# A hybrid encoder block on one Trainium2 core: 26 pairs of input projection blocks by one level of Strassen's recursion, in a stage of their own ahead of the DeltaNet heads

## Chip, core and metric

The kernel runs on one core of one Trainium2 chip. A core has TensorE (PE, matrix products), VectorE (DVE), ScalarE (ACT), GpSimd (POOL) and SyncE (SP), which here only issues DMAs; each works through its own queue of instructions in order, and waits on semaphores for the others. The metric is the device time of one execution in microseconds (us), lower is better.

## The reference, cut to what matters

x is 1024 tokens by 1024 channels, everything in float32. The input projection makes ten groups of 1024 channels (and 32 small ones for decays):

```python
h = rmsnorm(x, norm_w[l]) * (1.0 + scale[:, None, :]) + shift[:, None, :]
proj = h @ w_in[l]
(a_bg, a_cg, a_x, a_z, q, k, v, z_b, a_raw, b_raw, gate_a_raw, gate_b_raw) = jnp.split(proj, split_pts, axis=-1)
ya = a_cg * dwconv_centred(a_bg * a_x, conv_a_w[l])
ya = (ya * jax.nn.silu(a_z)) @ w_pa[l]
...
o = gated_delta_chunked(q2, k2, v2, g2, b2)     # 8 heads, both directions, chunks of 64 tokens
...
yb = (o * jax.nn.silu(z)).reshape(bsz, slen, VAL_DIM).astype(dt_) @ w_pb[l]
merged = jax.nn.sigmoid(gate_a_raw) * ya + jax.nn.sigmoid(gate_b_raw) * yb
x = x + gate[:, None, :] * (merged @ w_o[l])
return rmsnorm(x, final_norm_w)
```

q, k and v go through a convolution of width 5, SiLU and (q, k) a normalisation before the heads.

## The kernel before, in words

**Products.** Each group of 1024 channels is eight blocks of 128, so the projection has 80 blocks. A float32 operand is split into a high part (a cast to fp32r on ACT) and a low part (operand minus high part), and a product is three matmuls: high by high, high by low, low by high. A block is 2 halves of 512 tokens x 8 slices of the inner dimension x 3 = 48 matmuls of 128x128 by 128x512. The weights of a block come as two loads (wr), two casts on ACT (wh) and two subtractions on POOL (wl). The hidden h stands in SBUF as hhi and hlo.

**Stages.** A prologue loads x and the adaLN weights, normalises, transposes, and makes the products of q, k, v of head 0 and k of head 1. Then come the eight heads, then the mixer's remaining blocks ("the ax stage", lines 1113 to 1158: bg, ax, cg of each slice, a convolution of width 3, and directly yhi and ylo), then the products with w_pa, w_pb and w_o.

**A head.** `prep_k(h)` transposes k, loads two tiles D (a row of decays, broadcast over 128 partitions, one tile for each direction), subtracts, takes the exponential, multiplies with the gram matrix into N, collects its 32x32 diagonal blocks by DMA through DRAM into the tile E, and inverts them on POOL in 30 steps of two operations (`et<-E` and `E<-E,et`); DMAs bring the result back (s, N, Vb). `prep_q(h)` makes the q side and turns v into vp. `chain(h)` completes the inversion on TensorE (psy, psu, psz, psv) and then goes through eight steps, each of which is a chain of small matmuls (cb, o) and operations on DVE (r, S) and ACT (vw, vn). `head_out(h)` normalises the output, multiplies with silu(z) and stores it in yb_d. D, N, qg, ktok have two buffers each: `prep_k(h)` asks for `chain_e` of head h-2 first, because D of head h-2 is an operand of its last o matmul.

**Fill.** While heads wait, TensorE works on projection blocks. The generator `fill()` hands them out, chosen by `choose()`: k, q, v of the coming heads and z when what they need is done, and otherwise one of 24 gate blocks (ga, gb, az), whose activated results go to DRAM. There are 52 such blocks in the heads.

**Order.** A scheduler written in Python (`Scheduler`, `Engine`) runs while the program is built: it estimates costs and hops between engines, and so fixes the order of instructions of every engine through the prologue and the heads. Nothing is decided at run time: an engine waits for the next instruction in its list. Engines other than TensorE are recorded in line 278, TensorE in line 200. After the heads, the order of the code stands, with a few priorities (`tc.high_priority`).

Of the kernel before, what the change touches and what calls it, by code (L numbers as in the profile page):

```python
# [8 lines left out]
F32 = mybir.dt.float32  # L9
# [15 lines left out]
START = 6  # L25
RESERVE = 4
HOPS = {'same': 0.15, 'other': 0.2, 'from pe': 0.4, 'to pe': 0.35}
# [6 lines left out]
LO_POOL = (2, 5)  # L34

# [7 lines left out]
class Slot:  # L43
    """What was done to a part of a tile: ends of reads, writes and memsets, and instructions not issued yet."""
# [6 lines left out]
class Scheduler:  # L51
    """Orders the instructions of all engines by an estimate of when they can run.

    Instructions of the engines other than TensorE are kept until their operands are there by the estimate, and then
    go to their engine by priority. Streams are generators that ask for TensorE instructions, PSUM banks, tiles and
    each other's marks; the first of them goes on whose next instruction can start at once, or else the one that can
    start first."""
# [126 lines left out]
    def step(self, stream):  # L184
        """Does what a stream asks for, and goes on to what it asks for next."""
# [65 lines left out]
class Engine:  # L251
    """Hands an engine's instructions to the scheduler."""
# [31 lines left out]
def block(ctx: ExitStack, tc: tile.TileContext, x, cT, wada, wadag, badaT, nwT, win, wab, cva, cvq,  # L284
# [10 lines left out]
    wp = pool("wp", 2)  # L295
# [22 lines left out]
    sza_d = dr.tile([8, P, T], F32, name="sza_d")  # L318
    sgb_d = dr.tile([8, P, T], F32, name="sgb_d")
    yb_d = dr.tile([8, P, T], F32, name="yb_d")  # L320
# [25 lines left out]
    def kmul(ps, w, k, half):  # L346
        wh, wl = (t[:, ch(k)] for t in w)
# [5 lines left out]
    weights, wanted, early = {}, [], {}  # L353
# [36 lines left out]
    ctx.enter_context(tc.manual_schedule(engines={nc.tensor.engine}))  # L390
    hctx = ctx.enter_context(ExitStack())
# [8 lines left out]
    gctx = ctx.enter_context(ExitStack())  # L400
    gctx.enter_context(tc.manual_schedule(engines={e.engine for e in (nc.vector, nc.scalar, nc.gpsimd, nc.sync)}))
    gc_ = gctx.enter_context(tc.tile_pool(name="gc", bufs=1))
# [9 lines left out]
    xpads = [gc_.tile([P, T + 4], F32, name=f"xpad{i}") for i in range(2)]  # L412
    for xp in xpads:
        G.memset(xp[:, 0:2], 0.0)
        G.memset(xp[:, T + 2 : T + 4], 0.0)
# [6 lines left out]
    with tc.tile_pool(name="st", bufs=1) as st:  # L422
# [34 lines left out]
        xnT = st.tile([P, KT, T], F32, name="xnT")  # L457
# [113 lines left out]
        def hidden():  # L571
            for k in range(KT):
                hx = yield tile_of(st, [P, T], "hx", f"hx{k}", 2)
# [5 lines left out]
                for half in range(n):  # L579
# [4 lines left out]
                    with urgent():  # L584
                        V.tensor_scalar(hx[:, sl], xnT[:, k, sl], mod[:, 2 * k : 2 * k + 1], mod[:, 2 * k + 1 : 2 * k + 2],
# [26 lines left out]

        def first_products():
            banks = yield from outer(((po, "k0"), (pp, "q0")))
            for i, name in enumerate(("k0", "q0")):
                for half in range(2):
                    S.activation(xpads[i][:, 2 + 512 * half : 514 + 512 * half], banks[name, half], AF.Copy)
                    yield free(banks[name, half])
# [19 lines left out]
        def next_products():  # L638
            yield "need", "x"
            banks = yield from outer(((pc, "v0"),))  # L640
            early["v0"] = [banks["v0", half] for half in range(2)]
            yield want(win[Q0 + 1], "q1")
            yield "need", ("w", "k1")
            early["k1"] = []
            for half in range(2):
                early["k1"].append((yield from product_of("k1", half, po)))
# [49 lines left out]
        sched.run([loads(), modulate(), hidden(), norm_x(), first_products(), decay_product(), decays(), next_products(), first_weights(), loader(0, 2)])  # L696
# [15 lines left out]

    npad = [0]
    tiles = {}

    def conv(h, name, ct0, tag, bufs, ready=None):
        xp = xpads[npad[0] % 2]
        npad[0] += 1
        for half in range(2):
            if ready is None or ready:  # L720
                ps = ready[half] if ready else (yield from product_of(f"{name}{h}", half))
# [8 lines left out]
    def activated(name, j, dst_d, func):  # L730
# [7 lines left out]
        Q.dma_start(dst_d[j], xp[:, 2 : T + 2])  # L738

    def silu_z(h):  # L740
        sz = yield big("tmp", f"sz{h}", 2)
        for half in range(2):
            ps = yield from product_of(f"z{h}", half)
            with urgent():
                S.activation(sz[:, ch(half, 512)], ps, AF.Silu)
            yield free(ps)
        tiles["z", h] = sz
        yield "mark", ("z", h)
# [278 lines left out]
    def head_out(h):  # L1027
        yield ("need", ("chain", h))
        yield ("need", ("z", h))
        sz, os_ = tiles["z", h], ghead[h]["vp"]  # L1030
# [9 lines left out]
    def fill():  # L1040
        jobs = []
        for h in range(H):
            if h > 1:
                jobs.append((K0 + h, f"k{h}", conv(h, "k", 8, "kT", 3), [("chain_e", h - 3)] if h >= 3 else []))
            if h > 1:
                jobs.append((Q0 + h, f"q{h}", conv(h, "q", 0, "qT", 3), [("chain_e", h - 3)] if h >= 3 else []))
            if h:
# [292 lines left out]
```

## Time and profile before

| | |
|---|---|
| times of three runs | 1515.09, 1521.39, 1522.44 us; median 1521.39 |
| profiled execution: span | 1511.0 us |
| what the median has around this span | 10.4 us |
| prologue up to the end of k1's product | 106.6 us |
| heads with their fill | to 965 us |
| ax stage | 965 to 1229 us |
| w_pa, w_pb, w_o stages | 1229 to 1319, to 1407, to 1511 us |

The profile page names busy time of each engine over the span (PE is TensorE's matmuls, PEld its weight loads), and the chain of waits followed back from the last instruction. A group of instructions is a line of the code, an engine, an operation and the tiles it writes and reads ("out<-in"), with its count, busy us, mean ns of one, and the idle time ahead of it. A tile's view gives the min, median and max duration of each kind of instruction in ns, and the first and last start in us. The windows view gives the busy time of all engines in stretches of the span.

### The profile page before, as it was taken

The numbers are of one execution on the slowest core, as the hardware profiler recorded it, in microseconds if no ns is written. First come the engines' busy times: TensorE is split into PE (matmuls) and PEld (weight loads), VectorE is DVE, ScalarE is ACT, GpSimd is POOL, SyncE is SP. The second block draws the span as 40 slices with busy tenths as digits, with TensorE's granted clock in tenths as the row PEclk, the third lists the DMA queues.
The fourth block names the chain that finished last, engine by engine and source line by source line (L and its number), as shares of the span: only waits on it lengthen the run. The fifth ranks groups of instructions, "written<-read, shape, count | busy, mean of one in ns | idle before, by whom it ended". The sixth has DMA issues, their size and how long they took to land.

```text
span 1511.0 us, 22593 instructions
## 1 busy us (share of the span) xinstructions
PE 1433.0 (95%) x8730; PEld 1196.2 (79%) x8730; DVE 735.0 (49%) x1382; ACT 549.8 (36%) x1308; POOL 645.2 (43%) x793
## 2 busy tenths in 40 slices
PE   5999999898999999989999999999999999999898
PEld 3787878787787878878878878888888888888686
DVE  7869334664853845647628422134443344122325
ACT  5226325663553654635535424211111112122211
POOL 6213894167184392671852931222222222355401
PEclk7899999999999999999999999999999999999999
DMA  8232332223314113222132121322222137344602
GB/s 327 83 109 64 112 98 57 71 70 98 84 44 134 35 56 127 57 78 84 59 103 70 57 84 44 125 97 80 74 86 96 56 120 256 133 130 143 229 20 98
DMA packets 90298, 149.15 MB, mean 99 GB/s; under 512 B 41424, under 2 KB 41808, under 8 KB 90192
## 3 DMA queue, kind: packets, MB, share of 16 engines
q1 hardware_dynamic: 89904, 146.94, 29.6%
q8 instruction: 68, 1.11, 0.3%
q10 hardware_dynamic: 288, 0.79, 0.1%
q14 instruction: 38, 0.31, 0.1%
HBM read 118.21 MB, written 29.49 MB: 98 GB/s over the span
## 4 chain that ended last, share of the span: by engine, by line
PE 54%; DVE 9%; POOL 8%; ACT 5%; DMA 4%; issue 2%; SPq 0%; POOLq 0%; ACTq 0%
PE pp_az L200 4%; PE pp_gb L200 3%; PE cb L200 3%; PE pp_k L200 3%; DMA mr<-m_d 2%; PE o L200 2%; POOL E L278 2%; PE pp_v L200 2%; POOL et L278 2%; PE pp_cg L1103 2%; PE pp_cg L1105 2%; PE pp_cg L1104 2%; PE pp_bg L1105 2%; PE pp_ax L1105 2%; PE pp_bg L1104 2%
## 5 line engine op out<-in xcount | busy, mean ns | idle before, releaser
L278 POOL TENSOR_TENSOR E<-E,et 64x30 f32<-64x30 f32 (+14 forms) x240 | 143.9, 600 | 17.1
L278 POOL TENSOR_TENSOR et<-E 64x30 f32<-64x30 f32 (+14 forms) x240 | 135.2, 564 | 17.2
L1138 DVE TENSOR_TENSOR axp<-pp_ax,bg 128x512 f32<-128x512 f32 x16 | 11.1, 692 | 111.1 <-PE pp_ax L1105 90.5
L278 ACT ACTIVATE vw<-cb,cols 128x128 f32<-128x128 f32 x112 | 36.2, 365 | 76.1 <-PE cb L200 75.7
L278 ACT ACT_TABLE_LOAD x47 | 60.3, 1283 | 1.6 <-PEq L1335 0.8
L278 DVE SCALAR_TENSOR_TENSOR vT<-xpad,cvq_t,vT 128x1024 f32<-128x1024 f32 x32 | 58.6, 1831 | 1.0
L1095 POOL TENSOR_TENSOR wl_ax<-wr_ax,wh_ax 128x512 fp32r<-128x512 f32 x16 | 27.3, 1724 | 68.2 <-ACT wh_ax L1094 68.2
L278 POOL TENSOR_TENSOR wl_q<-wr_q,wh_q 128x512 fp32r<-128x512 f32 x16 | 22.0, 1390 | 72.2 <-ACT wh_q L278 67.4
L200 PE MATMUL pp_z<-hhi,wl_z 128*128 128x512 f32 x128 | 52.2, 408 | 0.0
L200 PE MATMUL pp_z<-hhi,wh_z 128*128 128x512 f32 x128 | 52.2, 407 | 0.0
L200 PE MATMUL pp_gb<-hlo,wh_gb 128*128 128x512 f32 x128 | 51.9, 406 | 0.0
L200 PE MATMUL pp_ga<-hhi,wh_ga 128*128 128x512 f32 x128 | 51.8, 405 | 0.0
L200 PE MATMUL pp_gb<-hhi,wh_gb 128*128 128x512 f32 x128 | 51.8, 405 | 0.0
L200 PE MATMUL pp_z<-hlo,wh_z 128*128 128x512 f32 x128 | 51.7, 404 | 0.0
L200 PE MATMUL pp_az<-hhi,wl_az 128*128 128x512 f32 x128 | 51.7, 404 | 0.0
L200 PE MATMUL pp_az<-hhi,wh_az 128*128 128x512 f32 x128 | 51.7, 404 | 0.0
L200 PE MATMUL pp_gb<-hhi,wl_gb 128*128 128x512 f32 x128 | 51.6, 403 | 0.0
L200 PE MATMUL pp_az<-hlo,wh_az 128*128 128x512 f32 x128 | 51.4, 402 | 0.0
L200 PE MATMUL pp_ga<-hlo,wh_ga 128*128 128x512 f32 x128 | 51.3, 401 | 0.0
L200 PE MATMUL pp_ga<-hhi,wl_ga 128*128 128x512 f32 x128 | 51.2, 400 | 0.0
L1104 PE MATMUL pp_pa<-ylo,wh_pa 128*128 128x512 f32 x128 | 50.8, 397 | 0.2 <-DVE ylo L1158 0.2
L1095 POOL TENSOR_TENSOR wl_pa<-wr_pa,wh_pa 128x512 fp32r<-128x512 f32 x16 | 21.9, 1388 | 68.1 <-ACT wh_pa L1094 68.1
(352 smaller groups left out, 4490.5 us busy)
## 6 DMA issues: line engine op xcount, KB each, us to landing
wada<-in_wada SPq DMA_DIRECT2D x16, 512.0 KB, 7.3
D<-gr_d SPq DMA_DIRECT2D x16, 512.0 KB, 5.9
xt<-in_x SPq DMA_DIRECT2D x8, 512.0 KB, 7.8
wr_k<-in_win SPq DMA_DIRECT2D x16, 256.0 KB, 2.6
wr_q<-in_win SPq DMA_DIRECT2D x16, 256.0 KB, 3.5
wr_v<-in_win SPq DMA_DIRECT2D x16, 256.0 KB, 2.6
wr_ga<-in_win SPq DMA_DIRECT2D x16, 256.0 KB, 2.9
qg<-er_d SPq DMA_DIRECT2D x8, 512.0 KB, 6.2
```

Source lines behind the costliest of these rows:

```text
L200: getattr(self.pe, what)(out, *ins, **kw)
L278: self._sched.record(self._name, lambda: real(*args, **kw), outs, ins, cost, extra, table, op == "memset")
L1095: G.tensor_tensor(lo[:, ch(q, 512)], raw, hi[:, ch(q, 512)].bitcast(F32), ALU.subtract)
L1103: PE.matmul(ps, wh, mhi[k][:, sl], start=k == 0, stop=False)
L1104: PE.matmul(ps, wh, mlo[k][:, sl], start=False, stop=False)
L1105: PE.matmul(ps, wl, mhi[k][:, sl], start=False, stop=k == KT - 1)
L1138: V.tensor_tensor(xp[:, 1 + 512 * half : 513 + 512 * half], ps, bg[:, ch(half, 512)], ALU.mult)
```

## The change

**Before the heads.** A new stage makes 26 pairs of blocks: four pairs of ga, three of gb, three of z, and for each of four positions a pair of bg, ax, cg and az. A pair is the product of 256 output channels with 1024 tokens, and is cut into 2x2 on each of its three dimensions: weights A11, A12, A21, A22 (slices of the inner dimension even or odd, since the rows of w_in are now laid out in the order KORDER), and B11 ... B22 of the hidden. The Winograd form of Strassen's recursion makes seven products of a quarter size in the place of eight: with the sums S1 to S4 of weights and T1 to T4 of the hidden, and sums of results. Each product is 4 slices x 3 = 12 matmuls, so a pair has 84 matmuls and not 96. For T1 to T4 the hidden is kept in float32 (xnT), and 16 sums on DVE, 16 casts on ACT and 16 low parts (11 on DVE, 5 on POOL) are made once. Each pair has 4 weight loads of 256 KB, 4 weight sums (DVE), seven casts (ACT) and seven low parts (POOL), made five products ahead (AHEAD). The results, activated, go to DRAM: sga_d, sgb_d, sz_d; and the mixer's whole result, after the convolution of width 3 and its multiplications, to y_d.

**Prologue.** The products of k0, q0, v0, k1 are copied to SBUF and stored to DRAM (raw_d), and loaded again as the heads start.

**Heads.** `fill()` has 24 blocks: q1, v1, and k, q, v of heads 2 to 7, and z and gb of positions 6 and 7 (TAIL) as spares. silu(z) is loaded from sz_d in `head_out`.

**After the heads.** The ax stage is gone. Eight tiles yr are loaded from y_d (two buffers), cast on ACT into yhi, and subtracted on DVE into ylo. The gate columns (wadag, ga) are made in the w_pa loop.

```diff
+    for m in range(4):
+        b11, b12, b21, b22 = (xnT[:, 2 * m + odd, ch(half, 512)] for odd in range(2) for half in range(2))
+        NV.tensor_tensor(b11, b12, b11, ALU.subtract)
+        NV.tensor_tensor(b12, b22, b12, ALU.subtract)
+        NV.tensor_tensor(b22, b22, b11, ALU.subtract)
+        NV.tensor_tensor(b21, b21, b22, ALU.subtract)
+        for n, t in zip(SUMS, (b22, b11, b12, b21)):
+            hi, lo = hop[n][m]
+            NS.activation(hi, t, AF.Copy)
+            (NG if lows % 3 == 2 else NV).tensor_tensor(lo, t, hi.bitcast(F32), ALU.subtract)
+            lows += 1
...
+    RHS = {"S2": "T2", "A11": "B11", "S1": "T1", "S3": "T3", "A12": "B21", "A22": "T4", "S4": "B22"}
...
+        def prep(self, n):
...
+            NS.activation(hi, t, AF.Copy)
+            NG.tensor_tensor(lo, t, hi.bitcast(F32), ALU.subtract)
+            self.ops[n] = hi, lo
+
+        def product(self, n):
...
+            for m in range(4):
+                mh, ml = hop[RHS[n]][m]
+                for i, (w, r) in enumerate(((hi, mh), (hi, ml), (lo, mh))):
+                    PE.matmul(ps, w[:, ch(m)], r, start=first and m == i == 0, stop=m == 3 and i == 2,
+                              skip_group_check=True)
+            self.after(n, ps)
...
+    pairs = [stored("ga", j, sga_d, AF.Sigmoid) for j in range(0, 8, 2)]
+    pairs += [stored("gb", j, sgb_d, AF.Sigmoid) for j in range(0, 8 - TAIL, 2)]
+    pairs += [stored("z", j, sz_d, AF.Silu) for j in range(0, 8 - TAIL, 2)]
+    pairs += [mixed(n, j) for j in range(0, 8, 2) for n in ("bg", "ax", "cg", "az")]
...
-        gates = [(G_A + j, f"ga{j}", activated("ga", j, sga_d, AF.Sigmoid), []) for j in range(8)]
-        gates += [(G_B + j, f"gb{j}", activated("gb", j, sgb_d, AF.Sigmoid), []) for j in range(8)]
-        gates += [(A_Z + j, f"az{j}", activated("az", j, sza_d, AF.Silu), []) for j in range(8)]
...
+        spare = [(Z0 + j, f"z{j}", activated("z", j, sz_d, AF.Silu), []) for j in range(8 - TAIL, 8)]
+        spare += [(G_B + j, f"gb{j}", activated("gb", j, sgb_d, AF.Sigmoid), []) for j in range(8 - TAIL, 8)]
...
-        yield from conv(0, "k", 8, "kT", 3, [])
+        yield from conv(0, "k", 8, "kT", 3, 0)
...
+    for k in range(KT):
+        raw = yp.tile([P, T], F32, tag="yr", name=f"yr{k}", bufs=2)
+        Q.dma_start(raw, y_d[k])
+        S.activation(yhi[k], raw, AF.Copy)
+        V.tensor_tensor(ylo[k], raw, yhi[k].bitcast(F32), ALU.subtract)
```

Three places show how the order moves. The first is ACT's list after the last product of the prologue, k of head 1 (pp_k). Before (xpad is the padded input of the convolution, wh the high part of a weight block, kT and qT the convolved k and q of head 0, ktp k's transposes):

```order
L278 ACTIVATE xpad_116<-v_1_721 128x512
L278 ACTIVATE wh_ga_889<-wr_ga_0_891 128x512
L278 ACTIVATE xpad_117<-pp_k_0_816 128x512
L278 ACTIVATE xpad_117<-pp_k_1_853 128x512
L278 ACT_TABLE_LOAD
L278 ACTIVATE kT_885<-kT_885 128x1024
L278 ACTIVATE wh_ga_889<-wr_ga_1_892 128x512
L278 ACTIVATE qT_886<-qT_886 128x1024
```

Now (raw is the copy for DRAM; T1h to T4h are the high parts of the sums of the hidden, whS and whA those of the weight sums and weights):

```order
L280 ACTIVATE raw_867<-pp_k_1_840 128x512
L728 ACTIVATE T2h_882<-xnT 128x512
L728 ACTIVATE T1h_890<-xnT 128x512
L728 ACTIVATE T3h_898<-xnT 128x512
L728 ACTIVATE T4h_906<-xnT 128x512
L728 ACTIVATE T2h_884<-xnT 128x512
...
L728 ACTIVATE T3h_904<-xnT 128x512
L728 ACTIVATE T4h_912<-xnT 128x512
L762 ACTIVATE whS_ga_984<-S_ga_982 128x512
L762 ACTIVATE whA_ga_988<-wr_ga_976 128x512
L762 ACTIVATE whS_ga_994<-S_ga_992 128x512
```

The casts of all sixteen sums stand between the copy of k1 and the first weight sum of the stage.

The second is TensorE's list in the last head's chain, in a late step. Before (cb, o: the chain's matmuls, pp_az: a fill block):

```order
L200 MATMUL cb7_0_8553<-r7_0_6_8784,N0_7_7517 128x128 [waits DVE_49]
L200 MATMUL cb7_1_8554<-r7_1_6_8786,N1_7_7518 128x128 [waits DVE_49]
L200 MATMUL pp_az4_1_8743<-hhi4_505,wl_az4_8426 128x512
L200 MATMUL pp_az4_1_8743<-hhi5_544,wh_az4_8425 128x512
L200 MATMUL pp_az4_1_8743<-hlo5_545,wh_az4_8425 128x512
L200 MATMUL pp_az4_1_8743<-hhi5_544,wl_az4_8426 128x512
L200 MATMUL pp_az4_1_8743<-hhi6_583,wh_az4_8425 128x512
L200 MATMUL pp_az4_1_8743<-hlo6_584,wh_az4_8425 128x512
L200 MATMUL pp_az4_1_8743<-hhi6_583,wl_az4_8426 128x512
L200 MATMUL cb7_0_8553<-vw7_0_6_8794,ktok7_7512 128x128 [waits Activation_49]
L200 MATMUL cb7_1_8554<-vw7_1_6_8796,ktok7_7512 128x128 [waits Activation_49]
L200 MATMUL o7_1_8552<-vn7_0_6_8797,D0_7_7515 128x128
```

Now:

```order
L202 MATMUL cb7_0_11114<-vw7_0_5_11247,ktok7_10033 128x128 [waits Activation_49]
L202 MATMUL cb7_1_11115<-vw7_1_5_11249,ktok7_10033 128x128 [waits Activation_49]
L202 MATMUL o7_1_11113<-vn7_0_5_11250,D0_7_10036 128x128
L202 MATMUL o7_0_11110<-vn7_1_5_11251,D1_7_10037 128x128
L202 MATMUL cb7_0_11114<-S7_0_5_11257,kT7_9780 128x128 [waits DVE_49]
L202 MATMUL cb7_1_11115<-S7_1_5_11259,kT7_9780 128x128 [waits DVE_49]
L202 MATMUL o7_1_11113<-S7_0_5_11257,qg0_7_10416 128x128
L202 MATMUL o7_0_11110<-S7_1_5_11259,qT7_9968 128x128
L202 MATMUL cb7_0_11114<-r7_0_6_11265,N0_7_10038 128x128 [waits DVE_49]
L202 MATMUL cb7_1_11115<-r7_1_6_11267,N1_7_10039 128x128 [waits DVE_49]
```

No fill matmul stands between the steps of head 7 any more; in the loops of the other heads there are 48 to 96.

The third is SP's list of DMAs at the end of the heads. Before (the store of the last head, then weights of the ax stage):

```order
L278 DMA yb_d<-sz_8424 128x1024
L278 DMA sza_d<-xpad_117 128x1024
L1093 DMA wr_bg_0_9092<-in_win 128x512
L1093 DMA wr_bg_1_9096<-in_win 128x512
L278 DMA sza_d<-xpad_116 128x1024
L1093 DMA wr_ax_0_9154<-in_win 128x512
L1093 DMA wr_ax_1_9158<-in_win 128x512
L278 DMA sza_d<-xpad_117 128x1024
```

Now (yr: the mixer's result, ybr: the heads', sga and sgb: gates):

```order
L280 DMA yb_d<-sz_10878 128x1024
L1275 DMA wr_pa_1_11590<-in_wpa 128x512
L280 DMA sz_11307<-sz_d 128x1024
L280 DMA yb_d<-sz_11307 128x1024
L1297 DMA yr_11367<-y_d 128x1024
L1297 DMA yr_11371<-y_d 128x1024
L1316 DMA wadag_11432<-in_wadag 128x1024
L1318 DMA sga_11434<-sga_d 128x1024
L1331 DMA ybr_11498<-yb_d 128x1024
L1318 DMA sga_11514<-sga_d 128x1024
L1331 DMA ybr_11580<-yb_d 128x1024
L1368 DMA sgb_12117<-sgb_d 128x1024
```

The loads of the mixer's result stand behind the last head's store, in turns with others.

More of the change, by code (lines that the diff above doesn't have):

```diff
@@ L615, in first_products @@
             for i, name in enumerate(("k0", "q0")):
-                for half in range(2):
-                    S.activation(xpads[i][:, 2 + 512 * half : 514 + 512 * half], banks[name, half], AF.Copy)
-                    yield free(banks[name, half])
+                yield from spill(i, banks, name)
         def decay_product():
@@ new lines, in block @@
+    tctx = ExitStack()
+    tctx.enter_context(tc.manual_schedule(engines=others))
+    tp = tctx.enter_context(tc.tile_pool(name="tp", bufs=1, reuse_waits="tile"))
+    bw = tctx.enter_context(tc.tile_pool(name="bw", bufs=1, reuse_waits="tile"))
+    SUMS = ("T2", "T1", "T3", "T4")
+    hop = {}
+    for i, n in enumerate(SUMS):
+        hop[n] = [[tp.tile([P, 512], F32R, name=f"{n}{p}{m}") for p in "hl"] for m in range(4)]
+    for n, odd, half in (("B11", 0, 0), ("B21", 1, 0), ("B22", 1, 1)):
+        hop[n] = [[t[2 * m + odd][:, ch(half, 512)] for t in (hhi, hlo)] for m in range(4)]
@@ L711, in conv5 @@
         S.activation(dst, dst, AF.Silu)
+    xpads = [gp.tile([P, T + 4], F32, name=f"xpad{i}") for i in range(2)]
+    for xp in xpads:
+        G.memset(xp[:, 0:2], 0.0)
+        G.memset(xp[:, T + 2 : T + 4], 0.0)
     npad = [0]
@@ L718, in conv @@
         npad[0] += 1
-        for half in range(2):
-            if ready is None or ready:
-                ps = ready[half] if ready else (yield from product_of(f"{name}{h}", half))
+        if ready is not None:
+            Q.dma_start(xp[:, 2 : T + 2], raw_d[ready])
+        else:
+            for half in range(2):
+                ps = yield from product_of(f"{name}{h}", half)
                 with urgent():
@@ L737, in activated @@
             yield free(ps)
[L738 to L748, printed above, removed]
+        Q.dma_start(dst[j], xp[:, 2 : T + 2])
+        yield "mark", (name, j)
     ghead = {}
@@ new lines, in block, with gate_column @@
+    bctx = ExitStack()
+    bp = bctx.enter_context(tc.tile_pool(name="bp", bufs=1, reuse_waits="tile", side="right"))
+    bhi = [bp.tile([P, T], F32R, name=f"bhi{k}") for k in range(KT)]
+    blo = [bp.tile([P, T], F32R, name=f"blo{k}") for k in range(KT)]
+    psm = bank(pc, "psg")
+    gsum = []
+    def gate_column(j):
+        PE.matmul(psm[:, j : j + 1], gsum[j], one)
+        V.tensor_tensor(gcol[:, j : j + 1], psm[:, j : j + 1], badaT_t[:, 16 + j : 17 + j], ALU.add)
+    with tc.tile_pool(name="bs", bufs=2, reuse_waits="tile", side="right") as bs:
@@ L1140, in block @@
-            V.tensor_scalar(acc, xp[:, 0:T], cva_t[:, j, 0:1], None, ALU.mult)
-            for i in range(1, 3):
-                V.scalar_tensor_tensor(acc, xp[:, i : i + T], cva_t[:, j, i : i + 1], acc, ALU.mult, ALU.add)
-            ga = ap.tile([P, P], F32, tag="ga", name=f"ga{j}")
+                ps = product(w, yhi, ylo, half, f"pa{j}")
+                V.tensor_tensor(sg[:, ch(half, 512)], ps, sg[:, ch(half, 512)], ALU.mult)
+            Q.dma_start(m_d[j], sg)
+            ga = bs.tile([P, P], F32, tag="ga", name=f"ga{j}")
```

292 lines of the change are left out of this document (191 added, 101 removed).

## The prediction

> **What bounds the kernel now.** The page comes first: the busy time of the engines and, in its fourth part, the shares of the chain that ended last.
>
> ```profile
> PE 1433.0 (95%) x8730; PEld 1196.2 (79%) x8730; DVE 735.0 (49%) x1382; ACT 549.8 (36%) x1308; POOL 645.2 (43%) x793
> PE 54%; DVE 9%; POOL 8%; ACT 5%; DMA 4%; issue 2%; SPq 0%; POOLq 0%; ACTq 0%
> ```
>
> TensorE is busy 95% of 1511.0 us, so fewer matmuls look like a gain. But the second row names it for only 54%: the heads contain a chain through DVE, ACT, POOL and DMA nearly as long as the work that covers it. So I read the stages next (windows view: stretch, its length, busy us and instructions of PE, PEld, DVE, ACT and POOL, granted clock, DMA share, GB/s).
>
> ```profile
> 20.00:35.00 15.00, 10.21 (x44) 8.24 (x45) 14.62 (x22) 6.92 (x12) 12.91 (x11) 0.50 0.96 372
> 35.00:50.00 15.00, 12.37 (x45) 9.93 (x44) 15.00 (x40) 4.16 (x7) 4.27 (x1) 0.60 0.53 171
> 479.00:580.00 101.00, 96.03 (x786) 81.47 (x786) 58.52 (x121) 51.94 (x133) 56.35 (x78) 1.00 0.26 78
> 965.00:1229.00 264.00, 264.00 (x1172) 218.70 (x1171) 106.00 (x141) 44.60 (x73) 68.76 (x52) 1.00 0.24 82
> 1229.00:1319.00 90.00, 89.79 (x386) 72.23 (x386) 27.73 (x27) 18.34 (x27) 22.72 (x17) 1.00 0.55 196
> 1319.00:1407.00 88.00, 88.00 (x395) 73.02 (x394) 21.26 (x28) 21.12 (x36) 44.12 (x35) 1.00 0.44 141
> 1407.00:1511.00 104.00, 90.97 (x417) 74.90 (x415) 41.19 (x68) 17.96 (x44) 21.07 (x21) 0.95 0.30 111
> ```
>
> TensorE is full in one head's period (479 to 580), in the ax stage (965 to 1229) and in the w_pa, w_pb and w_o stages. The price of a matmul comes from the chain of waits (start, us, what); the end of the prologue from the tile view of pp_k, between 85 and 240 us (ns min/median/max, first and last start in us).
>
> ```profile
> 560.95 10.91 PE pp_gb L200 x48
> L200 PE MATMUL pp_k<-hhi,wl_k x16: 388/390/393, 95.8 to 106.2; 128*128 128x512 f32 x16
> ```
>
> One block is 48 matmuls in 10.91 us, 0.2273 us each; the k1 product ends at 106.6, the heads' fill at 965. What the heads cost without fill is read from three tile views: head 0 (between 85 and 240 us), head 4's preparation (430 to 600) and head 4's chain (575 to 640).
>
> ```profile
> L278 DVE TENSOR_SCALAR kT<-xpad,cvq_t x2: 741/744/748, 95.2 to 111.2; 128x1024 f32<-128x1024 f32 x2
> L278 DVE SCALAR_TENSOR_TENSOR kT<-xpad,cvq_t,kT x8: 1273/1275/2320, 96.6 to 120.4; 128x1024 f32<-128x1024 f32 x8
> L278 POOL MEMSET E<- x2: 153/158/162, 144.7 to 172.7; 64x32 f32 x2
> L278 SPq DMA_DIRECT2D s<-E x2: 465/468/470, 206.7 to 238.9; - x2
> L200 PE MATMUL psy<-T,N x32: 192/237/258, 214.8 to 218.9; 32*32 32x32 f32 x32
> ...
> L278 SPq DMA_DIRECT2D D<-gr_d x2: 376/400/424, 474.3 to 476.7; - x2
> L278 DVE SCALAR_TENSOR_TENSOR D<-D,gcm,maskF x8: 343/346/347, 497.0 to 501.2; 128x128 f32<-128x128 f32 x8
> L278 POOL MEMSET E<- x1: 156/156/156, 519.6 to 519.6; 64x32 f32 x1
> L278 SPq DMA_DIRECT2D s<-E x1: 455/455/455, 570.1 to 570.1; - x1
> L200 PE MATMUL psy<-T,N x64: 190/192/213, 479.3 to 580.0; 32*32 32x32 f32 x64
> L200 PE MATMUL psy<-T,N x32: 190/192/213, 579.5 to 580.0; 32*32 32x32 f32 x32
> L200 PE MATMUL o<-vn,D x32: 270/276/276, 594.9 to 636.1; 128*128 128x128 f32 x32
> ```
>
> The D tiles are the hinge. There are two buffers for each direction, head h keeps its own until its last o matmul, and prep_k(h+2) may ask for them only then. From that moment: the load of D, the work from the first D operation (497.0) to the inversion's MEMSET (519.6), the inversion to its store (570.1), psy (579.5), the last o (636.1). In this kernel seven fill blocks lie between psy of heads 3 and 4 (479.3 and 579.5), so a head takes 100.2 us; without the 7 x 10.91 = 76.4, a head has only 24 us of TensorE work of its own. Two periods, 200 us, are longer than the D-to-D chain, so nobody sees that chain today.
>
> **The change, part by part.** *Prologue.* Spilling k0, q0, v0, k1 to DRAM adds casts and four stores behind products; the product of k1 still ends at 106.6 (bounds 106 to 109).
>
> *Start of the Strassen stage.* TensorE needs the low part of the first weight sum. Ahead of it ACT does all sixteen casts of T1 to T4 behind the last copy of k1's product, DVE twelve of the sixteen sums and eleven lows, then two weight sums. The nearest rows are these, from the groups by line.
>
> ```profile
> L1220 DVE TENSOR_TENSOR mlo<-mr,mhi 128x512 fp32r<-128x512 f32 x16 | 14.3, 896 | 54.3 <-ACT mhi L1219 54.3
> L278 ACT ACTIVATE wh_ga<-wr_ga 128x512 fp32r<-128x512 f32 x16 | 10.0, 625 | 16.6 <-DMA wr_ga<-in_win 7.6 <-POOL et L278 4.7 <-PE pp_k L200 4.2
> L1095 POOL TENSOR_TENSOR wl_ax<-wr_ax,wh_ax 128x512 fp32r<-128x512 f32 x16 | 27.3, 1724 | 68.2 <-ACT wh_ax L1094 68.2
> ```
>
> DVE: 12 + 11 + 2 = 25 operations x 0.896 = 22.4; then a cast 0.6 and a low 1.7: about 25 us (12, if most of DVE's share fits under the k1 product; 30, if POOL's lows hold it up). In it TensorE has nothing, as its order goes straight from k1 to the first Strassen product.
>
> *Strassen stage.* 26 pairs x 7 products x 12 matmuls = 2184, x 0.2273 = 496 us, against 26 x 96 x 0.2273 = 567 before: 71 us gone, the whole saving. Per pair (19.1 us) POOL does seven lows, 7 x 1.72 = 12.1; ACT seven casts and some copies, about 8; DVE five weight sums and the output sums, 7 to 19. So TensorE should set the pace, DVE nearly so where the mixer's pairs run.
>
> A matmul starts every 227.3 ns in the quoted chain. The Trainium skill, "TensorE: Matmul & The Clock Gate", section "Wait — 56ns, not 53.3ns?", gives 215.7 ns for 512 columns on the full clock; by it the stage would be 471 us, 25 less. The measured row decides, as these matmuls alternate with weight loads in the same pattern.
>
> *Heads.* Three loads of 512 KB stand in the page's sixth part (KB each, us to landing).
>
> ```profile
> D<-gr_d SPq DMA_DIRECT2D x16, 512.0 KB, 5.9
> xt<-in_x SPq DMA_DIRECT2D x8, 512.0 KB, 7.8
> ybr<-yb_d SPq DMA_DIRECT2D x8, 512.0 KB, 5.8
> ```
>
> Head 0's preparation no longer runs beside ten fill blocks. k0 is first reloaded (512 KB; xt took 7.8), and its five convolution operations (0.74 + 4 x 1.28 = 5.9) share DVE with those of q0, v0, k1 and q1. Before, it took 49.5 from the first of these (95.2) to E (144.7), 62 for the two interleaved inversions (to 206.7) and 8.1 to psy (214.8). With 8 for the reload and 8 for the mixing, psy of head 0 is about 136 after Strassen's end (120 to 145). In that time TensorE has four of 24 blocks (q1, v1, k2, q2; buffers stop it there) and some 12 us of small work, 56 in all, so some 80 are idle.
>
> After that the D-to-D chain paces it: load 5.9, 497.0 to 519.6 = 22.6, inversion 50.5, store to psy 9.4, psy to the last o 56.6; sum 145. Fewer weight lows between the inversion's operations (three blocks a head for seven) take off some 4: 141 for two heads, 70 each.
>
> So psy of head 0 at 136, of head 1 some 50 later (its loop has 48 fill matmuls, less than before), of head 7 three cycles of 141 later, 609; its loop without a single fill matmul takes 45 instead of 56.6 to the last o: 654 us for the stage. TensorE's own work in it is only 24 x 10.91 + 8 x 24 = 454. The cover that 28 gate and z blocks gave has been spent ahead of the heads; that is where the saving is lost.
>
> *After the heads.* Before, the mixer's blocks followed on TensorE without a gap while yhi and ylo were made one by one. Now yr0 stands on SP behind the store yb_d of head 7, which waits for DVE at the chain's end; eight loads with two buffers alternate with others, twenty 512 KB loads to yr7. At 372 GB/s (the best window above) 10.5 MB take 28; the store, the last cast and low, and three waits for a free buffer bring it to about 41 (25 to 50). Behind SP's wait nothing else that TensorE needs can pass; the w_pa weights are already there. The w_pa stage then has 87 of products, of which some 5 go under the loads: 82. Its extra work (the gate columns) hides under TensorE: DVE was busy 27.7 of its 90 us. From 1319 to the end nothing changes: 192.
>
> *Sum.* 106.6 + 25 + 496 + 654 + 41 + 82 + 192 = 1597. The profiled execution of before had 1511.0 of span; the median of the three runs is 1521.39, so 10.4 lie around it: 1607 us. A measurement of this kernel tells about 0.5% from no change, 7.6 us.
>
> **The rivals.** *TensorE stays the bound of the heads.* The order has fill in every loop but the last; if the preparation of head h+2 fits beside chain h+1, a cycle of two heads is set by matmuls, about 100. Then the stage is 654 − 3 x 41 = 531, the time 1484: faster. It decides at a cycle of 112: there 3 x 29 = 87 are won back and the kernel is level (1520); below 110 it is faster. For it: the inversion's 50.5 held six weight lows and the other chain's operations, and POOL is 56% busy in that window. Against: the sum consists of steps that wait for each other, all measured in a full machine where DVE was at 58%; they would have to shrink by a fifth. 0.06 faster; 0.03 more for a mixture that lands within 0.5%.
>
> *The clock drops.* Between 20 and 35 us TensorE had sparse transposes and the granted clock was 0.50, in the next 15 us still 0.60. After the change each chain has idle stretches of 10 us and more. If the work after each of about nine such stretches loses between nothing and the 0.4 x 15 = 6 us of that second window, the middle is 9 x 3 = 27 us: 1634. The Trainium skill, same page, section "Part 1: The HAM clock gate", states such a rule: half clock after an idle window of about 3.4 us, the full one again after as long of work. By that rule, the two rows agree in kind; no row of before shows a heads stage with gaps. 0.15.
>
> *DVE or POOL sets the Strassen stage.* The first of these rows is a subtraction of the ax stage, the second one of the same shape in the w_pa stage.
>
> ```profile
> L1158 DVE TENSOR_TENSOR ylo<-acc,yhi 128x1024 fp32r<-128x1024 f32 x8 | 9.8, 1226 | 9.0 <-ACT yhi L1157 9.0
> L1179 DVE TENSOR_TENSOR blo<-ybr,bhi 128x1024 fp32r<-128x1024 f32 x8 | 13.6, 1717 | 6.9 <-ACT bhi L1178 6.9
> ```
>
> The same subtraction takes 40% longer in other company. With seven lows a pair on POOL, the sixteen mixer pairs (19 us of DVE at the lower price) would run at 22 to 23: 16 x 3.5 = 56 more, 1663. The Trainium skill, "SBUF — State Buffer", section "Who interferes with whom", says that a DVE instruction with two SBUF inputs contends with a GpSimd one that reads SBUF; the two rows fit that. 0.12.
>
> **How the numbers follow.** My forecast with its own bounds (start 12 to 30, head 0's psy 120 to 145, cycle 130 to 148, loads 25 to 50) has 0.64 and reaches from about 1550 to 1640. The range takes in the clock and part of the DVE case, 1545 to 1660. Faster 0.06, within 0.5% 0.03, slower 0.91.
>
> **What would show it.** In the profile after: PE below 90%, its busy time 71 us lower; the Strassen stage about 496 long with PE full; psy starts of heads two apart 141 us apart, with D's load issued just after the last o of two heads before; an idle TensorE of some 80 us before the first psy and 40 before the first pa block. I am wrong if psy of consecutive heads come 50 to 55 apart, if DVE is full in the Strassen stage, or if TensorE goes from the last chain to pa without a gap.

## The result and the profile after

The changed kernel takes 1685.51 us in the median of four runs (1680.33 to 1686.99), the kernel before 1518.87 beside it: a ratio of 1.109, 95% interval 1.106 to 1.112. The direction was the one forecast. The size was not: 1607 with a range up to 1660 was given, so 78 us are missing from the sum.

The page after, busy time and the chain that ended last:

```profile
PE 1420.3 (85%) x8418; PEld 1175.7 (70%) x8418; DVE 923.0 (55%) x1677; ACT 586.7 (35%) x1390; POOL 781.2 (47%) x876
PE 12%; DMA 3%; POOL 1%; DVE 1%; issue 1%; ACT 1%; POOLq 0%; SPq 0%
```

There are 312 matmuls fewer, which at 0.2273 us each are 71 us, but TensorE's busy time falls by 12.7 and not by the 71 of the forecast. Busy time is not a count of work: in this trace a matmul of one and the same kind in the w_pa stage (pp_pa<-yhi,wh_pa) is busy for 388 to 796 ns. TensorE's share of the span falls from 95% to 85%, while the span grows by 167.5 us, from 1511.0 to 1678.5. DVE has 188 us more to do and GpSimd 136. The chain is of little use here: it is followed back only through the last fifth of the span. The stages say where the time is. The windows view of the kernel after: the end of the prologue, the wait for the first sums, the Strassen stage, head 0's preparation, the eight chains, and the w_pa stage with its loads.

```profile
0.00:110.00 110.00, 85.65 (x386) 69.58 (x386) 73.29 (x156) 36.82 (x59) 31.23 (x39) 0.88 0.42 152
110.00:134.00 24.00, 0.11 (x1) 0.00 (x0) 20.93 (x27) 9.83 (x19) 6.79 (x9) 0.55 0.33 110
134.00:653.00 519.00, 503.96 (x2184) 414.49 (x2184) 255.72 (x328) 160.21 (x269) 242.21 (x186) 0.98 0.22 75
653.00:791.00 138.00, 64.76 (x272) 51.97 (x272) 82.91 (x137) 42.67 (x97) 85.82 (x113) 0.71 0.25 79
791.00:1355.00 564.00, 484.64 (x4360) 413.19 (x4360) 360.97 (x820) 268.08 (x820) 329.32 (x459) 0.93 0.26 75
1355.00:1487.00 132.00, 101.12 (x411) 78.27 (x410) 66.67 (x117) 30.36 (x50) 20.15 (x16) 0.83 0.55 195
```

The second row is a stage that did not exist: 24 us in which TensorE does nothing and DVE is busy for 21. The fourth is head 0's preparation, with TensorE idle for more than half of it. For the kernel before, the same view of its heads (its ax stage and the stages behind it stand in the prediction):

```profile
106.00:965.00 859.00, 815.61 (x5985) 688.87 (x5984) 458.42 (x960) 411.21 (x1072) 451.02 (x624) 0.99 0.26 80
```

From this comes the account, in us of the two profiled executions:

| stage | before | after | difference | forecast of after |
|---|---|---|---|---|
| to the end of k1's product | 106.6 | 110.1 | +3.5 | 106.6 |
| wait for the first sums | – | 24.0 | +24.0 | 25 |
| Strassen stage | – | 518.6 | +518.6 | 496 |
| heads, to the last o | 859 | 702.5 | −156.5 | 654 |
| ax stage | 264 | – | −264 | – |
| loads of the mixer's result, w_pa | 90 | 131.7 | +41.7 | 41 + 82 = 123 |
| to the end | 192 | 191.6 | 0 | 192 |

The differences add up to 167.3 of the 167.5. Two terms carry the miss: the heads with 48.5 and the Strassen stage with 22.6; the w_pa stage adds 8.7, the prologue 3.5. A small one goes the other way: the forecast put 10.4 us around the span, and here the median lies 7.0 above it. Every execution on record takes only 1.7 to 2.1 us more than its own span; the rest of such a difference is that the profiled execution was quicker than the median one.

The hinge of the forecast is visible in two tile views: o of head 2 (955 to 1003 us), and D around head 4's load (985 to 1035), with the load, the first and the last operation on it.

```profile
L202 PE MATMUL o<-vn,D x32: 275/275/580, 955.0 to 999.5; 128*128 128x128 f32 x32
```

```profile
L280 SPq DMA_DIRECT2D D<-gr_d x2: 326/348/370, 999.5 to 999.9; - x2
L280 DVE SCALAR_TENSOR_TENSOR D<-D,gcm,maskF x8: 344/346/352, 1005.2 to 1011.4; 128x128 f32<-128x128 f32 x8
L280 DVE SCALAR_TENSOR_TENSOR N<-gram,cols,D x16: 341/342/351, 1016.1 to 1020.5; 128x128 f32<-128x128 f32 x16
```

Head 2's last o starts at 999.5, and the loads of D are issued at 999.5 and 999.9. It is so for the first of the two loads in all six heads that reuse a buffer (within 0.6 us); the second follows it by less than 1 us, in head 6 by 11. In the kernel before, the same load came at 474.3, 39 us after head 2's last o; the same view there (391 to 445):

```profile
L200 PE MATMUL o<-vn,D x32: 271/275/276, 394.4 to 435.3; 128*128 128x128 f32 x32
```

The cycle of two heads is 157 us, though, not 141: psy starts at 791.4, 846.3, 935.2, 1004.6, 1096.5, 1167.3, 1262.5 and 1318.7.

### The profile page after: what moved, and what is told of

Its sections match the earlier page's. It is cut to its first block, busy times and chain, and to the rows that moved or that the text cites. A ratio compares the mean times of both kernels' runs of the same rounds, so it can differ in the third digit from the quotient of the medians.

```text
span 1678.5 us, 22701 instructions
## 1 busy us (share of the span) xinstructions
PE 1420.3 (85%) x8418; PEld 1175.7 (70%) x8418; DVE 923.0 (55%) x1677; ACT 586.7 (35%) x1390; POOL 781.2 (47%) x876
## 5 line engine op out<-in xcount | busy, mean ns | idle before, releaser
L1285 PE MATMUL pp_pa<-yhi,wh_pa 128*128 128x512 f32 x128 | 53.9, 421 | 19.9 <-ACT yhi L1298 19.8
L280 DVE SCALAR_TENSOR_TENSOR kT<-xpad,cvq_t,kT 128x1024 f32<-128x1024 f32 x32 | 53.4, 1667 | 0.6
L202 PE MATMUL pp_q<-hhi,wh_q 128*128 128x512 f32 x112 | 47.6, 425 | 7.1 <-ACT wh_q L280 7.1
L1287 PE MATMUL pp_pa<-yhi,wl_pa 128*128 128x512 f32 x128 | 52.3, 409 | 0.0
L1285 PE MATMUL pp_pb<-bhi,wh_pb 128*128 128x512 f32 x128 | 49.9, 390 | 0.0
L1287 PE MATMUL pp_pb<-bhi,wl_pb 128*128 128x512 f32 x128 | 49.8, 389 | 0.0
L1286 PE MATMUL pp_pb<-blo,wh_pb 128*128 128x512 f32 x128 | 49.8, 389 | 0.0
L202 PE MATMUL pp_q<-hhi,wl_q 128*128 128x512 f32 x112 | 47.7, 426 | 0.1
L202 PE MATMUL pp_v<-hhi,wh_v 128*128 128x512 f32 x112 | 47.8, 427 | 0.0
L202 PE MATMUL pp_v<-hlo,wh_v 128*128 128x512 f32 x112 | 47.3, 423 | 0.0
```

Source lines behind the costliest of these rows:

```text
L202: getattr(self.pe, what)(out, *ins, **kw)
L280: self._sched.record(self._name, lambda: real(*args, **kw), outs, ins, cost, extra, table, op == "memset")
L1285: PE.matmul(ps, wh, mhi[k][:, sl], start=k == 0, stop=False)
L1286: PE.matmul(ps, wh, mlo[k][:, sl], start=False, stop=False)
L1287: PE.matmul(ps, wl, mhi[k][:, sl], start=False, stop=k == KT - 1)
```

## Experiments

The theory after the result: the 28 blocks that left the heads had been cheap there, because the heads have a slow chain of their own, paced by D's two buffers; Strassen's saving is real and small beside that. The rivals: GpSimd's inversions or DVE's queue set the pace of the heads; TensorE does and the Strassen sums disturb the kernel; the clock.

**Strassen alone: eight plain products in the same stage.** The sums of the hidden, of weights and of results are gone, everything else stays:

```diff
-    RHS = {"S2": "T2", "A11": "B11", "S1": "T1", "S3": "T3", "A12": "B21", "A22": "T4", "S4": "B22"}
+    RHS = {"A11": "B11", "A12": "B21", "A21": "B11", "A22": "B21", "a11": "B12", "a12": "B22", "a21": "B12", "a22": "B22"}
```

> The changed kernel with the same 26 pairs in the same stage, but by the eight plain products of a pair (96 matmuls) and without any sums of the hidden, the weights or the results. It separates Strassen from the move. Theory (the move costs, Strassen saves less than its 71 us): the stage takes 567 of matmuls, starts some 20 us earlier and has no waits for sums, ends about 28 later than now; heads unchanged at 702; time about 1713. Rival (the sums disturb the whole kernel so much that Strassen costs time by itself): the time is below 1685.

Measured: 1714.70 us (ratio 1.129, 1.127 to 1.131), as the theory had it, within 2 us. The windows of this kernel: the stage and the heads.

```profile
114.00:682.00 568.00, 567.64 (x2496) 469.40 (x2496) 62.36 (x71) 101.11 (x177) 132.87 (x108) 1.00 0.21 72
682.00:1386.00 704.00, 550.34 (x4632) 464.49 (x4632) 446.34 (x955) 309.93 (x916) 413.42 (x571) 0.88 0.25 75
```

TensorE is full for 568 us and the stage starts 20 us sooner; the heads take 704 against 702.5. So the recursion by itself wins 29 us of the 71 that its missing matmuls are worth, and the rest of the change (the move of the blocks, with the stores and reloads that it needs) costs about 195.

**What the gate blocks cost where they were.** This is the kernel before; the matmuls and activations of ga, gb and az are left out, their weights still come.

```diff
-        for half in range(2):
-            ps = yield from product_of(f"{name}{j}", half)
...
         Q.dma_start(dst_d[j], xp[:, 2 : T + 2])
```

> The kernel before the change with the matmuls and activations of the 24 gate blocks (ga, gb, az) left out of the heads; their weights are still loaded and split, and something is stored in their place, so the output is not the reference's. It measures what these blocks cost where they were: 24 x 10.91 = 262 us of TensorE. Theory (the heads have a chain of their own of some 600 to 700 us beneath the fill, so a fill block costs far less there than its matmuls; from 702 us with 24 blocks to 859 with 52 it is 5.6 us each): the heads fall by about 134, the time from 1519 to about 1385. Rival (TensorE sets the heads, so each block costs its 10.91): the time is about 1260.

Measured: 1418.77 us, 99 less than the kernel before beside it (ratio 0.935, 0.932 to 0.937). The heads' window, and the ax stage behind it:

```profile
106.00:869.00 763.00, 600.97 (x4832) 507.44 (x4832) 440.26 (x959) 352.70 (x999) 464.73 (x630) 0.89 0.30 91
869.00:1133.00 264.00, 264.00 (x1170) 218.63 (x1169) 107.36 (x143) 42.58 (x69) 66.34 (x46) 1.00 0.25 80
```

TensorE lost 215 us of busy time by its records, and the stage only 96: 4.0 us for a block whose matmuls take 10.91. That is less than the 5.6 that the theory gave, and far from the rival's 10.91. Two limits belong to the number. The weights of these blocks were still loaded and split, so it is the price of matmuls and activations alone. And some three of the blocks had stood behind the last o, from 933.5 to 965, at full price; up to the last o (now at 860.5) the heads fall by 73, which is 3.5 for each of the other 21. A block of a pair costs half of 518.6 / 26, 10.0 us, in the Strassen stage. Taking 12.5% off a block's matmuls and paying for the rest in full is dear for blocks that were two thirds hidden.

**Gates back into the heads.** Only the 16 mixer pairs stay in the stage:

```diff
-    pairs = [stored("ga", j, sga_d, AF.Sigmoid) for j in range(0, 8, 2)]
-    pairs += [stored("gb", j, sgb_d, AF.Sigmoid) for j in range(0, 8 - TAIL, 2)]
-    pairs += [stored("z", j, sz_d, AF.Silu) for j in range(0, 8 - TAIL, 2)]
-    pairs += [mixed(n, j) ...
+    pairs = [mixed(n, j) ...
+            spare.append((Z0 + j, f"z{j}", activated("z", j, sz_d, AF.Silu), []))
+            spare.append((G_A + j, f"ga{j}", activated("ga", j, sga_d, AF.Sigmoid), []))
+            spare.append((G_B + j, f"gb{j}", activated("gb", j, sgb_d, AF.Sigmoid), []))
```

> The changed kernel with only the 16 mixer pairs in the Strassen stage; ga, gb and z, 24 blocks, are fill of the heads again (20 blocks more than in the changed kernel, 20 x 10.91 = 218 us of TensorE). Theory (lost cover: TensorE idles some 250 us in the heads): the Strassen stage is 10 x 19.1 = 191 shorter, the heads grow by only 20 to 70 from 702, the time is 1520 to 1570. Rival (the heads are bound by TensorE's order, so each block adds its time): the heads grow by 218, the time is about 1710.

Measured: 1617.57 us (ratio 1.066, 1.063 to 1.068): 68 less than the changed kernel, and neither number. The windows of its heads, and of the fill that is left over after the last chain, with the first loads of the w_pa stage:

```profile
464.00:1232.00 768.00, 688.00 (x5324) 578.79 (x5325) 448.81 (x954) 360.69 (x987) 437.55 (x599) 0.95 0.28 87
1232.00:1304.00 72.00, 61.63 (x278) 50.43 (x277) 7.28 (x16) 22.61 (x47) 16.94 (x13) 0.95 0.40 137
```

The last chain ends at 1232, but five spare blocks stand behind it, with no chain to hide under. With these 56 us the heads take 825, 122 more for 20 blocks: 6.1 each. The direction is the theory's. Up to the last o the heads grow by 66 us for the fifteen blocks that stand there, 4.4 each with their weights' preparation, near what the gate experiment gives; the other five have their full price, because this simple order put them behind the last chain.

**A third buffer for D, N and ktok.**

```diff
-        if h >= 2:
-            yield ("need", ("chain_e", h - 2))
+        if h >= 3:
+            yield ("need", ("chain_e", h - 3))
...
-            D.append((yield big(f"D{d}", f"D{d}_{h}", 2)))
+            D.append((yield big(f"D{d}", f"D{d}_{h}", 3)))
```

> The changed kernel with a third buffer for D, N and ktok, so that the preparation of head h+2 may start before the chain of head h has ended (room for it: one buffer for v, silu(z) in the tile of er, vw in the tile of r). Theory (the heads are paced by the refill of D, 157 us for two heads): the cycle falls towards two chains plus what lies between them, 2 x 62, the heads from 702 to about 620, the time from 1685 to about 1605. Rival (GpSimd's inversions with the weight lows, or the order of the chain itself, set the pace): the heads stay within 15 us of 702, the time at 1670 to 1700.

Measured: 1675.44 us (ratio 1.103, 1.101 to 1.105), by its number the rival's. But psy of the first four heads come at 793.8, 847.6, 910.7 and 973.4, from the second on 63 apart, as the theory had it; the next is at 1078.6. In the order that was built, from head 4 on D's load stands behind k of that head, which stands in the fill behind v of the head before, and that v waits for prep_q of the one before it. So, it seems, the wait for D was gone and the next wait was right behind it. To tell these apart, the same kernel with the order of the fill changed:

```diff
+        turn = {"k": -1.4, "q": -0.6, "v": -0.3}
+        jobs.sort(key=lambda job: int(job[1][1:]) + turn[job[1][0]])
```

> The kernel with three buffers for D (e1_d3) and the fill blocks in another order: k of head h+1 ahead of v of head h, which waits for prep_q of head h-1. Theory (with D free, the preparation of heads 4 and later starts late because their k stands behind a v that waits): psy of heads 3 and 4 come some 80 apart instead of 105, the heads fall from 692 to about 650, the time from 1675 to about 1635. Rival (the chain of small operations on DVE, ACT and GpSimd is the limit whatever comes first): within 15 us of 1675.

Measured: 1641.56 us (ratio 1.083, 1.079 to 1.086), near the theory's 1635; psy of heads 3 and 4 are 70 apart. Two tile views of this kernel: the last o of head 2 (928 to 980 us), and psy of head 3 (960 to 980).

```profile
L202 PE MATMUL o<-vn,D x32: 275/275/275, 930.9 to 971.1; 128*128 128x128 f32 x32
```

```profile
L202 PE MATMUL psy<-T,N x32: 191/191/212, 973.2 to 973.7; 32*32 32x32 f32 x32
```

psy follows 2 us after the last o of the head before, and so in all heads from the first to the last (2 to 7 us). The chains stand end to end, and the heads take 655. D's two buffers and the fill's order behind them thus hold 47 us of the 702; what is left is 130 of preparation and eight chains of some 65 us.

**Weight lows on DVE in the heads.**

```diff
-                (G if LW[q] == "g" else V).tensor_tensor(lo[:, ch(q, 512)], raw, ...
+                (V if heads else G).tensor_tensor(lo[:, ch(q, 512)], raw, ...
```

> The changed kernel with the low parts of the heads' weights made on DVE instead of GpSimd (48 subtractions of 128x512). Theory (the inversions take 50 to 56 us and not 41 because weight lows stand between their steps): each inversion is some 8 us shorter, a cycle of two heads falls from 157 to about 148, the heads by some 25, the time is about 1660. Rival (DVE's queue is as tight as GpSimd's: what the inversion wins, the D and N operations lose): the time stays within 10 us of 1685, with the inversions shorter and the stretch from D to E longer.

Measured: 1672.24 us (ratio 1.102, 1.099 to 1.104), between the two. The tile view of E for head 4, first in the kernel after (1025 to 1097 us), then in this one (1015 to 1075):

```profile
L280 POOL MEMSET E<- x1: 160/160/160, 1030.2 to 1030.2; 64x32 f32 x1
L280 SPq DMA_DIRECT2D s<-E x1: 461/461/461, 1086.0 to 1086.0; - x1
```

```profile
L280 POOL MEMSET E<- x1: 159/159/159, 1020.0 to 1020.0; 64x32 f32 x1
L280 SPq DMA_DIRECT2D s<-E x1: 461/461/461, 1067.2 to 1067.2; - x1
```

55.8 us against 47.2; over heads 2 to 7 the mean falls from 50.2 to 44.9. The stretch from D's load to E grows by 2 us in the mean (from the last o to E by 5, as two of the six loads come some 10 us later), and the heads are 11 shorter. GpSimd's lows had a part, a small one.

**First priority for the work on D.**

```diff
+        with urgent():
             for d in range(2):
                 for c in range(NC):
                     V.scalar_tensor_tensor(D[d][:, ch(c)], D[d][:, ch(c)], ...
```

> The changed kernel with the operations of prep_k on D, N and Vc on DVE and ACT given the scheduler's first priority (otherwise they stand between convolutions and the scaling of the head before). Theory (the cycle of two heads is 157 and not 141 because the stretch from the last o to E takes 36 us in the mean and not 28.5, with DVE's other work between its operations): the stretch falls to about 29, the heads from 702 by 20 to 40, the time to about 1655. Rival (what is put back, the chain of the other head or the next k, q, v, is as urgent): the heads within 10 us of 702.

Measured: 1689.40 us (ratio 1.114, 1.112 to 1.117), nothing won. The heads take 710. The stretch from D's load to E falls by 2 us in the mean, and from the last o to E by less than 1; the inversions are 2 longer (51.9 for 50.2). The rival holds: what was put back on DVE was about as urgent as what went ahead.

**Depth of preparation in the Strassen stage.** Four waits of up to 3.8 us (14.2 in all) stand in it, all at the same place. TensorE, DVE and ACT around the first (timelines of the kernel after: start, us, what, and the idle time ahead with its releaser):

```profile
377.79 0.50 PE L776 MATMUL ps_cg_S<-T3h,whS_cg 128*128 128x512 f32 x1 [3.75 <-DVE u_cg L789]
```

```profile
373.62 1.28 DVE L857 SCALAR_TENSOR_TENSOR acc<-axp,cva_t,acc 128x1024 f32<-128x1024 f32 x1
374.82 0.68 DVE L757 TENSOR_TENSOR S_cg<-wr_cg,S_cg 128x512 f32<-128x512 f32 x1
377.05 0.69 DVE L789 TENSOR_TENSOR u_cg<-ps_cg_S,e_cg 128x512 f32<-128x512 f32 x1 [1.54 <-ACT e_cg L787]
```

```profile
375.90 0.63 ACT L762 ACTIVATE whS_cg<-S_cg 128x512 fp32r<-128x512 f32 x1 [9.52 <-DVE S_cg L757]
376.43 0.58 ACT L787 ACTIVATE e_cg<-ps_cg_A 128x512 f32<-128x512 f32 x1
```

The result sum u must be read out of the bank before TensorE's next product may go into it. u waits for e, the copy of another bank; e stands on ACT behind the cast of a weight sum; and that sum stands on DVE behind the mixer's convolution. The first idea was to prepare weights earlier:

```diff
-AHEAD = 5
+AHEAD = 7
```

> The changed kernel with weights prepared seven products ahead instead of five. Theory (four waits of 3.8 us in the Strassen stage come from the weight sum S3 of cg, which stands on DVE behind 13 us of the width-3 convolutions): the sum is then ahead of them, the four waits go, the stage is about 15 shorter (518 to 503), the time about 1670. Rival (the waits come from busy DVE and GpSimd as such): the stage stays within 5 us.

Measured: 1752.16 us (ratio 1.153, 1.150 to 1.156), 67 slower than the changed kernel. The rows of the waits of TensorE and DVE in the stage of this kernel (who, for whom: us in total, times, longest):

```profile
PE ps_cg_S L776 <- DVE u_cg L789: 16.7, 4, 4.2
DVE u_ax L789 <- ACT e_ax L787: 16.2, 4, 4.1
PEld ps_bg_S L776 <- DVE u_bg L789: 16.1, 4, 4.3
```

The waits at cg are still there, and now ga, gb, z and bg have them too: with seven ahead, e stands behind casts of the next pair's sums. Those sums are late as well, for seven ahead is a whole pair, and a sum may wait for the next pair's weights:

```profile
DVE S_gb L757 <- DMA wr_gb<-in_win: 19.0, 4, 6.6
```

In the kernel after, the same wait is 0.2 us. The theory was wrong about the sum S3 of cg; it seems to be e's place in ACT's list that costs. If so, fewer products ahead must help:

```diff
-AHEAD = 5
+AHEAD = 4
```

> The changed kernel with weights prepared four products ahead instead of five. After the run with seven ahead, the theory is: the copy e of the first product's bank stands on ACT behind the cast of a weight sum that was prepared ahead of it, and that sum stands on DVE behind the mixer's convolutions; with four ahead the cast behind which e stands is that of a weight itself (A22), so e comes earlier and each of the four waits shrinks from 3.8 to about 1.6 us: the stage from 518.6 to about 510, the time from 1685 to about 1676. Rival (the depth of preparation is what hides the sums, so four ahead is worse, as fewer low parts are ready): the stage is longer than 518.

Measured: 1679.80 us (ratio 1.108, 1.106 to 1.110). The stage is 513.7 long, and the four waits take 10.9 us in place of 14.2. At the first wait, ACT and DVE now do this:

```profile
372.25 0.60 ACT L787 ACTIVATE e_cg<-ps_cg_A 128x512 f32<-128x512 f32 x1 [0.92 <-PE ps_cg_A L776]
```

```profile
372.61 4.40 DVE L857 SCALAR_TENSOR_TENSOR acc<-axp,cva_t,acc 128x1024 f32<-128x1024 f32 x2
376.93 0.68 DVE L789 TENSOR_TENSOR u_cg<-ps_cg_S,e_cg 128x512 f32<-128x512 f32 x1
```

The two medians are not clear of each other (ratios 1.106 to 1.110 here, 1.106 to 1.112 for the changed kernel), so the stage's length has to tell. Its direction agrees with the place on ACT: e starts at 372.3 here, at 376.4 in the changed kernel. The size is about half of what was expected, because u itself still stands behind the convolution.

```profile
PE ps_cg_S L776 <- DVE u_cg L789: 10.9, 4, 2.7
```

**The repairs together.** Third buffers, k first, lows on DVE, four ahead.

> The changed kernel with three buffers for D and k first (e7), the heads' weight lows on DVE (e5) and four products ahead (e8) together. If the three gains come from different waits, they add: 1642 - 13 - 6, about 1623. If the chains of the eight heads, which in e7 follow each other without a gap (70 us each), are now the limit, then shorter inversions win nothing and only the 6 of the Strassen stage are left: about 1636. Either way it stays above 1518, the kernel before.

Measured: 1638.43 us (ratio 1.080, 1.077 to 1.083), the second branch: with the chains end to end, shorter inversions win nothing (the heads take 659, against 655 in the run with k first). Of the 167 us lost, 47 come back. No version here beats the kernel before.

## Why the forecast was right and where it was wrong

**The direction and its cause: right.** "The cover that 28 gate and z blocks gave has been spent ahead of the heads; that is where the saving is lost" is what the experiments show: a block's matmuls were worth 4.0 us in the heads (3.5 to 4.4 under the chains), and they cost 10.0 in the stage, while the recursion by itself gains 29. By the table the 28 blocks cost 279 us in the stage, and the heads are 156.5 shorter, 5.6 a block: 123 lost. The first sums add 24, the loads 42, the prologue 3.5; the mixer's 24 blocks, at 10.0 instead of 11.0, win 25. That is the 167. Why the heads gave 5.6 a block and not 4.0 was not tried by itself. Here the preparation of the weights left the heads with the blocks; against that, the reloads of the prologue's products came in.

**Terms that held.** The wait for the first sums (25 forecast, 24.0), head 0's psy (136 after the Strassen stage, 138.7), psy of head 1 50 later (54.9), and everything from the w_pb stage on. Idle TensorE before the first psy was forecast at 80 and is 73. The last head's loop without fill takes 36.2 and not 45, which is 9 in the forecast's favour.

**The cycle of two heads: mis-sized.** 141 was forecast from rows of head 4 before, and 157 came, three times over: 49 us, the largest part of the 78. By parts, the mean of heads 2 to 7 after against the forecast: load of D to E 36.2 for 28.5, inversion 50.2 for 46.5, its store to psy 11.3 for 9.4, and psy to the last o 58.4 for 56.6 (heads 2 to 6, as head 7 has no fill). Half of the 16 thus lies between D's load and E: from the first operation on D to E it is 31.4 in the mean, where the row of head 4 gave 22.6 and the mean of the same heads before was 23.1. So the row was not an odd one. The sixteen operations on D alone stretch over 10 to 23 us in heads 2 to 7, where they stretched over 5 to 7. The step of the prediction that failed is the sum of the D-to-D chain ("sum 145", then "141 for two heads"): it added the durations of a chain from a trace in which nobody waited for it, and gave nothing for what else would fall on DVE at that time. In the new kernel the end of one head, the D work of the next but one and convolutions share DVE, which was busy 53% of the heads before and is busy 64% from the first psy on. The deduction of 4 us for fewer weight lows was wrong outright: lows on DVE show that GpSimd's still cost some 5 us an inversion. Beyond that no single wait was found that holds the 16 us; giving D's work priority only moved it. Where they lie is measured; their cause stays open.

**That D's buffers set the cycle: right, but not alone.** The loads of D follow the last o at once. With the buffers gone, the fill's order took their place; with that gone too, the chains themselves did, at 655. The idea of the first of these runs, that a free D would bring the heads to 620, was wrong.

**Strassen's 496: mis-sized by 22.6.** "TensorE should set the pace, DVE nearly so where the mixer's pairs run" was not followed through. By the starts of the matmuls, four waits at cg are 14.8; another 7.5 lie in 39 matmuls that start 0.3 to 0.6 us apart (most 0.43) instead of 0.227, ten of them at the start of the stage and the others behind those waits. The rival in which DVE or GpSimd sets the whole stage did not come: DVE is busy 256 of 519, and the stage lost 22, not the 56 that this rival put on it.

**The clock: smaller than its rival's price.** In the heads after, 36 fill matmuls are followed by the next one after 0.40 to 0.46 us, which is 7 us more than at the full rate, against the 27 given; in the heads before there are 18, with 3.6. The chain's own matmuls are little longer (o 285 ns in the mean for 275, the sixteen of gram in a head 340 for 278). From these means I estimate 1 to 2 us of a cycle, so the clock does not make the 16. The windows of low granted clock, 110 to 134 and 653 to 791 (0.55, 0.71), are those in which TensorE idles most. Behind the 24 us the windows show how it comes back:

```profile
134.00:138.00 4.00, 3.45 (x7) 2.33 (x8) 2.27 (x2) 2.63 (x6) 3.88 (x3) 0.50 0.00 0
138.00:142.00 4.00, 4.00 (x16) 3.20 (x14) 0.00 (x0) 0.63 (x1) 4.00 (x4) 0.80 0.00 0
142.00:146.00 4.00, 4.00 (x19) 3.34 (x18) 1.98 (x3) 0.91 (x2) 1.61 (x2) 1.00 0.00 0
```

Half the clock up to about 140 and the full one after, which agrees with the rule of the Trainium skill ("TensorE: Matmul & The Clock Gate", "Part 1: The HAM clock gate"): half when idle, full after some 3.4 us of work, by a window that does not start with the kernel. Here it was full after 5.6 us of work, and the half rate cost some 2.8. Behind three of the four waits at cg seven or eight matmuls start 0.43 us apart, which costs some 1.5 us a time.

**After the heads.** The loads were forecast at 41 with 82 behind them. An idle TensorE of 40 was forecast; measured, its first product starts 16 after the last o and then waits for one tile after the other. yhi is made from 1370.0 to 1397.7.

```profile
L1298 ACT ACTIVATE yhi<-yr x8: 1056/1057/1059, 1370.0 to 1397.7; 128x1024 fp32r<-128x1024 f32 x8
```

The eighth tile's low part is ready at 1400.0, 45 us after the last o and not 41. By then 22 of the stage's 384 matmuls have started, which are the 5 us that were taken to go under the loads. The other 362 take 87 to the end of the stage and not 82: the first ones start at half the rate, and the sixteen small matmuls of the gate columns stand between them. The granted clock of the whole window is 0.83.

## What to carry to other kernels

The price of an instruction is the price in its stage. Before work is taken from under a chain to be done faster elsewhere, leave it out once and see what the stage gives back: here 4.0 us for blocks whose matmuls take 10.9, so a recursion that saves an eighth of them could not pay for moving them. And when a covered chain becomes the bound, its length is not the sum of its steps as they were measured under cover: steps of different heads that never met now meet on one engine.

## What the runs showed of the hardware

The same operation on GpSimd took about three times as long while DVE ran convolutions. Two rows of GpSimd's timeline in the kernel after, operations of one form in two inversions (a late step of head 5's, an early one of head 6's):

```profile
1151.83 1.34 POOL L280 TENSOR_TENSOR et<-E 64x130 f32<-64x130 f32 x1
...
1199.10 0.40 POOL L280 TENSOR_TENSOR et<-E 64x130 f32<-64x130 f32 x1
```

and what DVE did at the first of them:

```profile
1149.99 4.26 DVE L280 SCALAR_TENSOR_TENSOR qT<-xpad,cvq_t,qT 128x1024 f32<-128x1024 f32 x3
```

1.34 is about one DVE operation of 1.42 us. In the seven other heads the step of the first row takes 0.47 to 0.54 us, with no convolution on DVE beside it. The step of the second row takes 0.40 to 0.41, except in head 1, where it stands beside a convolution and takes 1.28. The Trainium skill, "SBUF — State Buffer", section "Who interferes with whom", says that a DVE instruction with two SBUF inputs contends with a GpSimd instruction that reads SBUF, and that the lock on the ports they share is exclusive. The step lengths fit that rule; no run here took the convolutions away to show it alone.
